# Sorting the rotated features of q and k into two chunks, and gathering the score operands in pieces

## The chip, the cores and the metric

The kernel runs on one core of a Trainium2 chip. The metric is the device time of one execution in microseconds (us). Three runs of the kernel before gave 603.58, 604.00 and 606.18 us, so its median is 604.0 us.

## The reference

It is a decoder trunk of two layers on one sequence of 256 tokens with 1024 features, all in float32. Only the first sub-layer, softmax attention with partial rotary, is touched. With 256 tokens there is one key block, so the block selection falls away and plain causal attention is left:

```python
xn = rmsnorm(h, attn_norm)                     # (1, 256, 1024)
q, k, v = split(xn @ w_qkv)                    # 16 heads of 64 features each
# partial rotary: only features 0..15 of a head's 64 are rotated
x1, x2, rest = x[..., :8], x[..., 8:16], x[..., 16:]
x = concat([x1 * cos - x2 * sin, x2 * cos + x1 * sin, rest])      # for q and for k
s = (q * 64**-0.5) @ k.T ; s = where(causal, s, -inf)
h = h + (softmax(s) @ v) @ w_o
```

A SwiGLU layer, an mLSTM mixer, another SwiGLU layer and a last norm follow. The order of the features within a head's q and k changes nothing in a score, as long as q and k have the same order.

## The kernel before

Float32 products are made of three matmuls on high and low parts: each weight tile `raw` (128x1024, 512 KB) is read by SP's queue, ScalarE casts its high part `wh`, VectorE subtracts the low part `wl`, and TensorE multiplies high by high, high by low and low by high (`mm3`). Four `raw` buffers and eight pairs `wh`, `wl` run ahead of TensorE; a load of `raw` waits until the `wl` of the tile four before it is made.

The attention has three stretches. First, `first_block` computes the first four 128-feature blocks of q and k ("chunks" 0 to 3, one PSUM bank each: k in one half, q in the other). Then the stream `main` runs: a list of generators gives TensorE one step at a time, and a queue of small jobs is kept by step number. A step is six matmuls of 256 columns or three of 512, whatever the generator. The generators stand in this order (`ORDER`): 16 steps of v for heads 0 to 7, 8 steps each of chunks 4, 5 and 6, `V1` steps of v for heads 8 to 15, 8 steps of chunk 7, the rest of v, then 28 steps of the output projection. After the stream one unit of 4 steps is left, so it is 96 steps in all.

Jobs are set by step numbers. Chunk c goes through `rotary`, then `stacks`; here a chunk holds two whole heads. `rotary` shuffles on VectorE, multiplies by the cosine table `Cr` on VectorE and by the sine table `Sr` on GpSimd, and adds on GpSimd. `stacks` copies the high part to a tile `u` on ScalarE, subtracts the low part on VectorE and gathers, with three DMAs for each head on SP's queue, a tile `stk` whose 128 rows hold high and low parts above each other (64 rows each, so a score needs two matmuls over 128 rows). Head h then has `scores` (S, four matmuls, at step 26 + 3h), `softmax`, `exps`, `recip`, `normalize` (VectorE and ScalarE in turn), `transposes` (T, three matmuls, 8 steps after the scores), `halves` and `lows_p`, and `values` (V, four matmuls, 14 steps after the scores).

VectorE, ScalarE and TensorE execute this stretch in the order in which the jobs were called; in the kernel before SP's order comes from a planner. Each engine works its list strictly in order: an instruction that waits holds everything behind it. The four PSUM banks of the tag `ps` are shared by the chunks' results, S, T and V; a chunk's bank is free once its `rotary` has read it, a head's S bank once `softmax` has.

Of the kernel before, what the change touches and what calls it, by code (L numbers as in the profile page):

```python
# [9 lines left out]
F32 = mybir.dt.float32  # L10
F32R = mybir.dt.float32r
# [5 lines left out]
P = 128  # L17
S = 256
# [4 lines left out]
LOOK = 4  # L23
A_LOOK = 4
ORDER = (0, 4, 5, 6, 1, 7, 1)
V1 = 4
WBUFS = 8
RAW = 4
LAG = 6
WARM = 16  # L30

A_D1, A_X, A_D2, A_N, A_D3, A_L, A_D4, A_O1, A_O2 = 0.5, 1, 3, 1, 1, 1.5, 0.5, 1, 1
A_O3, A_D5, A_D6, A_E, A_R, A_S, A_S2, A_W = 1, 2, 0, 1, 5, 6, 1.5, 1
A_START, A_STEP, A_T, A_V = 26, 3.0, 8, 14
M_START, M_STEP, M_A, M_B, M_C, M_G2, M_G3 = 32, 5, 1.5, 12, 22, 23, 28


C_COS, C_SIN, C_AMASK, C_ID = 0, 256, 512, 768
# [42 lines left out]
def trunk_kernel(ctx: ExitStack, tc: tile.TileContext, x, w, wg, fw, tab, out):  # L81
    nc = tc.nc
# [23 lines left out]
    vector_scalar = {mybir.EngineType.DVE, mybir.EngineType.Activation}  # L106
# [20 lines left out]
    tab_t = const.tile([P, C_END], F32, name="tab_t")  # L127
# [53 lines left out]
    tcos = tab_t[:, C_COS:C_COS + S]  # L181
# [252 lines left out]
    n = n0 = Norm(V_ATTN)  # L434
# [45 lines left out]
    with ExitStack() as actx:  # L480
        ap = actx.enter_context(tc.tile_pool(name="attn", bufs=3))
        ap1 = actx.enter_context(tc.tile_pool(name="attn1", bufs=1))

        Cr = ap1.tile([P, S], F32, name="Cr")
        Sr = ap1.tile([P, S], F32, name="Sr")
        nc.gpsimd.tensor_mul(Cr, tcos, n.R)
        nc.gpsimd.tensor_mul(Sr, tsin, n.R)
        pad(ap1, 16)
        VT = ap1.tile([P, 2, 16, P], F32R, name="VT")
        swap = [8 + i if i < 8 else i - 8 if i < 16 else i for i in range(32)]  # L490
        st = {}

        def rotary(hp, bank):
            b3 = bank.rearrange("p (g t) -> p g t", g=2)
            qk = ap.tile([P, 512], F32, name="qk", tag="qk", bufs=2)
            sh = ap.tile([P, 512], F32, name="sh", tag="sh", bufs=2)
            qk3, sh3 = (a.rearrange("p (g t) -> p g t", g=2) for a in (qk, sh))
            nc.vector.stream_shuffle(sh, bank, swap)
            nc.vector.tensor_mul(qk3, b3, Cr.unsqueeze(1).to_broadcast([P, 2, S]))  # L499
            nc.gpsimd.tensor_mul(sh3, sh3, Sr.unsqueeze(1).to_broadcast([P, 2, S]))  # L500
            nc.gpsimd.tensor_add(qk, qk, sh)

            def stack():
                st[hp] = stacks(ap, qk, 3, later=lambda f: main.later(A_S2, lambda: (f(), stacked.add(hp))))
            main.later(A_S, stack)

        evicted = set()
        stacked = set()
# [19 lines left out]
        pr = {}  # L528

        def scores(h):  # L530
            T = st[h // 2][:, h % 2]
            sc = ps_tile()
            dots(sc[:, 0:P], T, 0, P, 0, P)
            dots(sc[:, P:384], T, P, P, 0, S)
            main.later(A_D1, softmax, h, sc)
# [87 lines left out]
        def qk(hp):  # L623
            b = ps_tile()
            yield from pair_block("aqk", hp, n, b)
            main.later(A_D5, rotary, hp, b)

        acc = []
        blocks = [tok_block("av", 2 * i, n, v_evict, lambda *a: main.later(A_D6, *a)) for i in range(2)]
        parts = {0: [blocks[0]], 1: [islice(blocks[1], V1), blocks[1]]}  # L630
        main = Stream(*[(always, parts[i].pop(0) if i < 4 else qk(i)) for i in ORDER],
                      ((lambda: 0 in ot and 1 in ot), out_start(acc, "ao", ot)), *[((lambda hp=hp: hp in ot), out_steps(acc, "ao", hp, ot)) for hp in range(2, 7)])
        for hp in range(4):
            main.at(A_R * hp, rotary, hp, banks[hp])
# [294 lines left out]
def _tables():  # L929
    import numpy as np  # L930

    t = np.zeros((P, C_END), np.float32)
    pos = np.arange(S, dtype=np.float32)
    inv = np.float32(500000.0) ** (-np.arange(0, 16, 2, dtype=np.float32) / np.float32(16))
    ang = pos[:, None] * inv.astype(np.float32)[None, :]
    cos, sin = np.cos(ang).T, np.sin(ang).T
    t[:, C_COS:C_COS + S] = 1.0
    for h in (0, 64):
        t[h:h + 8, C_COS:C_COS + S] = cos
        t[h + 8:h + 16, C_COS:C_COS + S] = cos  # L940
        t[h:h + 8, C_SIN:C_SIN + S] = -sin
        t[h + 8:h + 16, C_SIN:C_SIN + S] = sin
    i, j = np.arange(P)[:, None], np.arange(P)[None, :]
    t[:, C_AMASK + P:C_AMASK + S] = np.where(j <= i, 0.0, -1e30)
    t[:, C_ID:C_ID + P] = np.eye(P)
    t[:, C_EMASK:C_EMASK + S] = np.tile(np.where(i <= j, 0.0, -30000.0), (1, 2))
    t[:, C_TRIU:C_TRIU + P] = i <= j
    t[:, C_TRIS:C_TRIS + P] = i > j
    for h in range(8):
        t[h, C_ID2 + h] = 1.0  # L950
        t[32 + h, C_ID2 + h] = 1.0
    return t


def _chunks(d):
    import numpy as np

    def cols(a, c0, c1):
        return a[:, c0:c1].reshape(8, P, c1 - c0).transpose(1, 0, 2)

    def pair(a, ca, cb, h):
        u = np.stack([cols(a, ca, ca + P), cols(a, cb, cb + P)], axis=2)
        return u[:, 4 * h:4 * h + 4].reshape(P, 1024)

    def wide(a, c0, i, h):
        k = (i % 2) * 4 + h * 2
        return cols(a, c0 + (i // 2) * 512, c0 + (i // 2) * 512 + 512)[:, k:k + 2].reshape(P, 1024)

    def rows(a, i, h):
        return a[(2 * i + h) * P:(2 * i + h + 1) * P]  # L970

    wq, wo = d["attn_w_qkv"][0], d["attn_w_o"][0]
    wi, wu = d["mlstm_w_in"][0], d["mlstm_w_out"][0]
    out = []
    pairs = {"aqk": (wq, 1024, 0), "mqk": (wi, 0, 512)}
    for l in range(2):
        pairs[f"gu{l}"] = (d["ffn_w_gate_up"][l], 0, 2816)
    for n, i, h in unit_names():
        if n.endswith("*"):
            a, ca, cb = pairs[n[:-1]]  # L980
            c = np.stack([a[i * P:(i + 1) * P, c0:c0 + 512].reshape(P, 4, P) for c0 in (ca, cb)], axis=2)
            c = c.reshape(P, 1024)
        elif n in pairs:
            a, ca, cb = pairs[n]
            c = pair(a, ca + i * P, cb + i * P, h)
# [12 lines left out]
        out.append(c)  # L998
    return np.stack(out)
# [32 lines left out]
```

## Time and profile before

| what | us |
|---|---|
| median of 3 runs | 604.0 |
| profiled execution | 604.25 |
| its span, first to last instruction | 602.5 |
| TensorE busy | 587.8 (98%) |
| VectorE busy | 415.6 (69%) |
| ScalarE busy | 340.3 (56%) |
| GpSimd busy | 71.0 (12%) |
| mean granted TensorE clock | 0.998 |

1.75 us of the profiled execution lie outside the span. Rows of a timeline give start, duration, engine, line, operation, output and inputs, the count of merged instructions, and in brackets how long the engine was idle before and what released it. The durations of pipelined matmuls overlap, so the time that one costs is read from the start of one row to the start of the next.

### The profile page before, as it was taken

How to read it: one execution, taken by the hardware profiler on the slowest of the kernel's cores; microseconds unless marked ns; L12 is line 12 of the kernel's file. 1: busy time of each engine (PE TensorE's matmuls, PEld its weight loads, DVE VectorE, ACT ScalarE, POOL GpSimd, SP SyncE). 2: the span in 40 equal slices, each digit the busy share in tenths (PEclk: the TensorE clock that was granted, in tenths of full speed). 3: DMA queues.
4: the chain of work that ended last, by engine and by line, in shares of the span. 5: the costliest groups of instructions: out<-in, count | busy, mean ns of one | idle time of the engine just before them, and what ended most of it. 6: DMA issues, size and time to landing. Idle time of an engine off the chain costs nothing.

```text
span 602.5 us, 11621 instructions
## 1 busy us (share of the span) xinstructions
PE 587.8 (98%) x4536; PEld 557.4 (93%) x4536; DVE 415.6 (69%) x674; ACT 340.3 (56%) x615; POOL 71.0 (12%) x77
## 2 busy tenths in 40 slices
PE   8997999999999999999999999999999999999995
PEld 7987888999999999999999878999999999999984
DVE  5999798796866666565487768868785656656522
ACT  7655899766644444445275467846664444444412
POOL 0464420041000000000032300113100000000000
PEclk9999999999999999999999999999999999999999
DMA  8869985458655556555428868332854555555401
GB/s 299 310 216 268 242 207 159 143 177 303 218 200 185 206 182 205 184 203 184 168 73 290 256 217 226 130 141 90 297 208 175 201 183 195 191 201 185 140 0 70
DMA packets 36630, 116.39 MB, mean 193 GB/s; under 512 B 4576, under 2 KB 7904, under 8 KB 36576
## 3 DMA queue, kind: packets, MB, share of 16 engines
q1 hardware_dynamic: 36144, 115.19, 58.3%
q8 instruction: 35, 0.57, 0.4%
q10 hardware_dynamic: 432, 0.47, 0.2%
q14 instruction: 19, 0.16, 0.1%
HBM read 105.15 MB, written 1.05 MB: 176 GB/s over the span
## 4 chain that ended last, share of the span: by engine, by line
PE 75%; DMA 8%; DVE 7%; ACT 5%; issue 3%; SPq 2%; POOLq 0%; POOL 0%; ACTq 0%; DVEq 0%
PE ps L191 43%; PE acc L191 31%; DMA raw<-w 4%; DMA stk<-u 3%; DVE wl L154 3%; ACT wh L164 1%; DVE u L462 1%; SPq L465 1%; SPq L466 1%; ACT xh L211 1%; ACT p L548 1%; DMA XV<-x 1%; PE ps L568 0%; ACT u L458 0%; DVE qk L499 0%
## 5 line engine op out<-in xcount | busy, mean ns | idle before, releaser
L154 DVE TENSOR_TENSOR wl<-raw,wh 128x1024 fp32r<-128x1024 f32 (+1 forms) x200 | 243.5, 1223 | 109.6 <-ACT wh L164 109.2
L164 ACT CAST wh<-raw 128x1024 fp32r<-128x1024 f32 (+1 forms) x200 | 205.6, 1034 | 178.0 <-PE ps L191 96.1
L191 PE MATMUL ps<-xh,wh 128*128 128x256 f32 x864 | 240.6, 278 | 0.0
L191 PE MATMUL ps<-xh,wl 128*128 128x256 f32 x864 | 239.5, 277 | 0.7 <-DVE wl L154 0.7
L191 PE MATMUL ps<-xl,wh 128*128 128x256 f32 x864 | 239.3, 277 | 0.0
L191 PEld LDWEIGHTS ps<-xh,wh 128*128 128x128 f32 x864 | 162.7, 188 | 1.4 <-ACT wh L164 0.4
L191 PEld LDWEIGHTS ps<-xh,wl 128*128 128x128 f32 x864 | 162.4, 188 | 1.2 <-DVE wl L154 1.1
L191 PEld LDWEIGHTS ps<-xl,wh 128*128 128x128 f32 x864 | 162.6, 188 | 0.7
L191 PE MATMUL acc<-hh,wh 128*128 128x256 f32 x176 | 48.6, 276 | 0.0
L191 PE MATMUL acc<-hl,wh 128*128 128x256 f32 x176 | 48.6, 276 | 0.0
L191 PE MATMUL acc<-hh,wl 128*128 128x256 f32 x176 | 48.6, 276 | 0.0
L657 DVE TENSOR_TENSOR tgu<-ps,R 128x512 f32<-128x512 f32 x42 | 28.6, 690 | 19.0 <-PE ps L191 19.0
L191 PE MATMUL acc<-wh,xh 128*128 128x512 f32 x96 | 39.0, 406 | 0.0
L225 POOL TENSOR_TENSOR ssum<-ssum,sq 128x512 f32<-128x512 f32 x9 | 16.2, 1806 | 186.9 <-issue 163.7
L191 PE MATMUL acc<-wh,xl 128*128 128x512 f32 x96 | 37.8, 393 | 0.0
L191 PE MATMUL acc<-wl,xh 128*128 128x512 f32 x96 | 37.7, 393 | 0.0
L191 PE MATMUL acc<-wh,hh 128*128 128x512 f32 (+1 forms) x92 | 35.5, 386 | 0.6 <-DVE yout L422 0.5
L191 PE MATMUL acc<-wh,hl 128*128 128x512 f32 (+1 forms) x92 | 35.4, 384 | 0.0
L191 PE MATMUL acc<-wl,hh 128*128 128x512 f32 (+1 forms) x92 | 35.3, 384 | 0.0
L191 PEld LDWEIGHTS acc<-hh,wh 128*128 128x128 f32 x176 | 33.0, 188 | 0.0
L191 PEld LDWEIGHTS acc<-hl,wh 128*128 128x128 f32 x176 | 33.0, 188 | 0.0
L191 PEld LDWEIGHTS acc<-hh,wl 128*128 128x128 f32 x176 | 33.0, 188 | 0.0
(182 smaller groups left out, 854.1 us busy)
## 6 DMA issues: line engine op xcount, KB each, us to landing
raw<-w SPq DMA_DIRECT2D x194, 512.0 KB, 4.2
stk<-u SPq DMA_DIRECT2D x24, 192.0 KB, 4.5
stk<-u SPq DMA_DIRECT2D x24, 128.0 KB, 4.3
stk<-u SPq DMA_DIRECT2D x24, 64.0 KB, 3.5
XV<-x SPq DMA_DIRECT2D x6, 128.0 KB, 5.8
tab_t<-tab SPq DMA_DIRECT2D x1, 708.0 KB, 7.3
raw<-w SPq DMA_DIRECT2D x4, 128.0 KB, 3.7
raw<-w SPq DMA_DIRECT2D x2, 256.0 KB, 4.6
```

The costliest lines, as they stand in the source:

```text
L154: nc.vector.tensor_sub(wl[:, sl], raws[c][:, sl], wh[:, sl].bitcast(F32))
L164: nc.scalar.copy(wh[:, sl], raws[c][:, sl])
L191: nc.tensor.matmul(o, lhsT=lhsT, rhs=rhs, start=start, stop=stop, skip_group_check=True)
L211: nc.scalar.activation(self.h[:, f], X[:, f], AF.Copy, scale=wc)
L225: eng.tensor_add(self.ssum, self.ssum, sq)
L462: nc.vector.tensor_sub(u[:, 512:1024], mv, u[:, 0:512].bitcast(F32))
L465: nc.sync.dma_start(out=st[0:64, hh].bitcast(F32), in_=u[r, 0:768].bitcast(F32))
L466: nc.sync.dma_start(out=st[64:128, hh, 0:512].bitcast(F32), in_=u[r, 512:1024].bitcast(F32))
L548: nc.scalar.activation(pt[:, sl], pt[:, sl], AF.Exp, bias=mx[:, t:t + 1], scale=-1.0, accum_out=ss[:, t:t + 1])
L657: nc.vector.tensor_mul(t.rearrange("p (g t) -> p g t", g=2), bank.rearrange("p (g t) -> p g t", g=2), n.R2())
```

## The change

The columns of the q and k weights are sorted on the host. Of each half of the heads (0 to 7, 8 to 15) the 16 rotated features of all eight heads come first and fill one chunk (chunks 0 and 4), and the 48 others of the eight heads fill three (1 to 3, 5 to 7). `rotary` needs the shuffle and four VectorE operations for chunks 0 and 4 alone; the other six chunks take one multiply. GpSimd has no part in it any more.

A head's rows now lie in two or three chunks, so its tile (`stz`, one of seven fixed tiles, in place of `stk`) is gathered in two or three pieces of 16, 32 or 48 rows with two DMAs each: 18 pieces for eight heads, 72 DMAs in place of 48. The last quarter of a tile's lower half is zero, which leaves out the product of the two low parts.

Scores stand at step 18 + 3.5h in place of 26 + 3h. The first part of v for heads 8 to 15 has 8 steps in place of 4 (`V1`), and chunk 7 comes 4 steps later. SP joins the engines that work in the order of the calls.

```diff
-A_O3, A_D5, A_D6, A_E, A_R, A_S, A_S2, A_W = 1, 2, 0, 1, 5, 6, 1.5, 1
-A_START, A_STEP, A_T, A_V = 26, 3.0, 8, 14
+A_O3, A_D5, A_D6, A_E, A_S, A_S2, A_S3, A_W = 1, 0.5, 0, 1, 1.5, 1.5, 2, 1
+A_R = (0, 2, 5, 8)
+A_START, A_STEP, A_T, A_V = 18, 3.5, 8, 14
+NT = 7
-        nc.gpsimd.tensor_mul(Cr, tcos, n.R)
-        nc.gpsimd.tensor_mul(Sr, tsin, n.R)
+        nc.vector.tensor_mul(CS, tab_t[:, C_COS:C_COS + 2 * S].rearrange("p (g t) -> p g t", g=2), n.R2())
+        stz = [ap1.tile([P, 768], F32R, name=f"stz{i}") for i in range(NT)]
+        for T in stz:
+            nc.gpsimd.memset(T[64:128, 512:768].bitcast(F32), 0.0)
+        def segments(h):
+            c, j = h // 8 * 4, h % 8
+            yield c, 16 * j, 16, 0
+            r, to = 48 * j, 16
+            while to < 64:
+                m = min(64 - to, P - r % P)
+                yield c + 1 + r // P, r % P, m, to
+                r, to = r + m, to + m
+            if c % 4:
+                nc.vector.tensor_mul(qk3, b3, n.R2())
+            else:
+                sh = ap.tile([P, 512], F32, name="sh", tag="qk", bufs=2)
+                nc.vector.stream_shuffle(sh, bank, swap)
+                nc.vector.tensor_mul(qk3, b3, Cr.unsqueeze(1).to_broadcast([P, 2, S]))
+                nc.vector.tensor_mul(sh3, sh3, Sr.unsqueeze(1).to_broadcast([P, 2, S]))
+                nc.vector.tensor_add(qk, qk, sh)
+            main.later(A_S, stack_high, c, qk)
+        def stack_high(c, qk):
+            u = ap.tile([P, 1024], F32R, name="u", tag="u", bufs=3)
+            nc.scalar.copy(u[:, 0:512], qk)
+            main.later(A_S2, stack_low, c, qk, u)
+        def stack_low(c, qk, u):
+            nc.vector.tensor_sub(u[:, 512:1024], qk, u[:, 0:512].bitcast(F32))
+            parts[c] = u
+            ...
+                    main.when(main.pos + d, lambda h=h: h < NT or h - NT in scored, stack, h)
+        def stack(h):
+            T = stz[h % NT]
+            for c, r, m, to in segments(h):
+                v = parts[c][r:r + m].bitcast(F32)
+                nc.sync.dma_start(out=T[to:to + m].bitcast(F32), in_=v[:, 0:768])
+                nc.sync.dma_start(out=T[64 + to:64 + to + m, 0:512].bitcast(F32).rearrange("p (b c) -> p b c", c=S),
+                                  in_=v.rearrange("p (b c) -> p b c", c=S)[:, 0::3])
-        with tc.manual_schedule(engines=vector_scalar):
+        with tc.manual_schedule(engines=vector_scalar | {mybir.EngineType.SP}):
```

SP's list early in the stream. Before, a weight load stands after each chunk's six DMAs of `stk`; the last row is the load of the stream's eleventh weight tile:

```order
L145 DMA raw_562<-w 128x1024
L467 DMA stk_558<-u_556 64x256 x2
L465 DMA stk_558<-u_556 64x768
L466 DMA stk_558<-u_556 64x512
L465 DMA stk_558<-u_556 64x768
L466 DMA stk_558<-u_556 64x512
L145 DMA raw_597<-w 128x1024
```

In the change, the last piece DMAs of the first seven heads (`stz_478` is head 6's tile, `stz_472` that of heads 0, 7 and 14), the load of the same eleventh weight tile, and what follows:

```order
L543 DMA stz_478<-u 16x768
L544 DMA stz_478<-u 16x2x256
L543 DMA stz_478<-u 48x768
L544 DMA stz_478<-u 48x2x256
L147 DMA raw<-w 128x1024
L543 DMA stz_472<-u 16x768
L544 DMA stz_472<-u 16x2x256
L543 DMA stz_472<-u 48x768
L544 DMA stz_472<-u 48x2x256
L147 DMA raw<-w 128x1024 x5
```

From head 0's first piece to the eleventh tile's load there are 32 piece DMAs and two other weight loads; before, 12 DMAs of `stk` and one load stand there.

ScalarE's list from the first copy to `u` on, before (`exps` are the L548 rows):

```order
L458 CAST u<-qk 128x512 [waits Pool_49]
L164 CAST wh<-raw 128x1024 [waits DMAHW4_49,Activation_49]
L458 CAST u<-qk 128x512 [waits Pool_49]
L164 CAST wh<-raw 128x1024 [waits DMAHW5_49,PE_49,Activation_49]
L458 CAST u<-qk 128x512 [waits DMAHW3_49,DMAHW2_49,DMAHW4_49,DMAHW1_49,DMAHW7_49,DMAHW0_49,Pool_49]
L164 CAST wh<-raw 128x1024 [waits DMAHW6_49,PE_49]
L517 ACTIVATE VT<-acc,r 128x4x2x64 [waits PE_49] x2
L164 CAST wh<-raw 128x1024 [waits DMAHW5_49]
L458 CAST u<-qk 128x512 [waits DMAHW3_49,DMAHW2_49,DMAHW6_49,DMAHW1_49,DMAHW7_49,DMAHW0_49,Pool_49]
L164 CAST wh<-raw 128x1024 [waits DMAHW4_49]
L548 ACTIVATE p,ss<-p,mx 128x256 [waits DVE_49]
```

And in the change (`exps` are the L591 rows):

```order
L527 CAST u<-qk 128x512 [waits DVE_49]
L166 CAST wh<-raw 128x1024 [waits DMAHW4_49,Activation_49]
L527 CAST u<-qk 128x512 [waits DMAHW2_49,DMAHW1_49,DMAHW5_49,DMAHW0_49,DMAHW6_49,DVE_49,Activation_49]
L166 CAST wh<-raw 128x1024 [waits PE_49] x2
L559 ACTIVATE VT<-acc,r 128x4x2x64 [waits PE_49,Pool_49]
L559 ACTIVATE VT<-acc,r 128x4x2x64 [waits PE_49]
L591 ACTIVATE p,ss<-p,mx 128x256 [waits DVE_49]
L591 ACTIVATE p,ss<-p,mx 128x128 [waits DVE_49]
L166 CAST wh<-raw 128x1024 [waits DMAHW1_49]
L591 ACTIVATE p,ss<-p,mx 128x256 [waits DVE_49]
L591 ACTIVATE p,ss<-p,mx 128x128 [waits DVE_49]
```

The copies to `u` of chunks 2 and 3 are the first and third of these rows. There are three `u` tiles. In both kernels the copy of a fourth chunk waits for DMAs that read an earlier one (DMAHW names the semaphore of a DMA); in the change all four copies stand ahead of the `VT` copies and of the first `exps`, and the fourth waits for the pieces of heads 0, 1 and 2 that come out of chunk 1.

## Rows read from the trace of the kernel before

**Rows 1.** The page's first part: busy us, share of the span and instructions.

```profile
PE 587.8 (98%) x4536; PEld 557.4 (93%) x4536; DVE 415.6 (69%) x674; ACT 340.3 (56%) x615; POOL 71.0 (12%) x77
```

**Rows 2.** Windows: stretch, length, busy us of each engine, clock, DMA share, GB/s.

```profile
45.00:60.00 15.00, 11.28 (x94) 10.65 (x93) 14.65 (x32) 8.57 (x18) 6.05 (x5) 1.00 0.91 270
```

**Rows 3.** Timeline of TensorE: the stream's first matmul and three that waited.

```profile
29.45 0.39 PE L191 MATMUL acc<-wh,xh 128*128 128x512 f32 x1
...
53.94 0.69 PE L191 MATMUL ps<-stk 128*128 128x128 f32 x4 [1.42 <-issue]
...
58.40 0.84 PE L568 MATMUL ps<-tab_t,p 128*128 128x128 f32 x3 [2.24 <-ACT p L558]
...
69.41 0.83 PE L568 MATMUL ps<-tab_t,p 128*128 128x128 f32 x3 [0.98 <-DVE qk L499]
```

**Rows 4.** Chain of waits, late attention: start us, us, what.

```profile
101.60 0.41 PE ps L191 x4
...
102.01 0.35 PE ps L568 x3
...
103.06 0.46 PE ps L191 x4
...
116.27 7.55 PE acc L191 x66
```

**Rows 5.** Timeline of VectorE, 27 to 54 us.

```profile
27.62 0.76 DVE L498 STREAM_SHUFFLE sh<-ps 128x512 f32<-128x512 f32 x1
...
36.20 2.32 DVE L154 TENSOR_TENSOR wl<-raw,wh 128x1024 fp32r<-128x1024 f32 x1
...
48.11 1.65 DVE L520 SCALAR_TENSOR_TENSOR VT<-acc,r,VT 128x256 fp32r<-128x256 f32 x4
...
49.68 1.21 DVE L154 TENSOR_TENSOR wl<-raw,wh 128x1024 fp32r<-128x1024 f32 x1
...
53.18 0.66 DVE L499 TENSOR_TENSOR qk<-ps,Cr 128x512 f32<-128x512 f32 x1
...
53.77 0.40 DVE L542 CUSTOM_DVE_ANT_0 p<-ps,tab_t 128x256 f32<-128x256 f32 x1
```

**Rows 6.** Timeline of ScalarE, 44 to 58 us.

```profile
44.31 1.26 ACT L517 ACTIVATE VT<-acc,r 128x512 fp32r<-128x512 f32 x2
...
48.61 0.62 ACT L458 CAST u<-qk 128x512 fp32r<-128x512 f32 x1 [2.09 <-DMA stk<-u]
...
54.22 0.51 ACT L548 ACTIVATE p<-p,mx 128x256 f32<-128x256 f32 x1 [3.76 <-DVE mx L542]
...
55.60 1.05 ACT L164 CAST wh<-raw 128x1024 fp32r<-128x1024 f32 x1 [0.40 <-DMA raw<-w]
...
57.95 0.80 ACT L558 ACTIVATE p<-p,ss 128x128 f32<-128x128 f32 x2
```

**Rows 7.** Timeline of GpSimd.

```profile
35.81 1.62 POOL L501 TENSOR_TENSOR qk<-qk,sh 128x512 f32<-128x512 f32 x1
```

**Rows 8.** Timeline of SP's queue: an issue is its row's duration.

```profile
3.79 0.33 SPq L143 DMA_DIRECT2D XV<-x  x1
...
50.81 0.59 SPq L466 DMA_DIRECT2D stk<-u  x1
...
51.45 0.60 SPq L467 DMA_DIRECT2D stk<-u  x1
...
335.44 1.18 SPq L466 DMA_DIRECT2D stk<-u  x1
```

**Rows 9.** DMA issues, 30 to 60 us: count, KB each, median us to landing.

```profile
raw<-w SPq DMA_DIRECT2D x8, 512.0 KB, 4.1
```

**Rows 10.** The tile stk, 34 to 56 us: its DMAs.

```profile
DMA to landing us min/median/max: 2.4/3.0/3.8
```

**Rows 11.** Timeline of TensorE at the start.

```profile
1.12 3.59 PE L118 MATMUL acc<-warm 128*128 128x256 bf16 x16 [1.12 <-POOL warm L115]
...
6.20 0.28 PE L191 MATMUL ps<-xh,wh 128*128 128x256 f32 x1
```

More of the change, by code (lines that the diff above doesn't have):

```diff
@@ L25 @@
 ORDER = (0, 4, 5, 6, 1, 7, 1)
-V1 = 4
+V1 = 8
 WBUFS = 8
@@ L482, in trunk_kernel @@
         ap1 = actx.enter_context(tc.tile_pool(name="attn1", bufs=1))
-        Cr = ap1.tile([P, S], F32, name="Cr")
-        Sr = ap1.tile([P, S], F32, name="Sr")
-        nc.gpsimd.tensor_mul(Cr, tcos, n.R)
-        nc.gpsimd.tensor_mul(Sr, tsin, n.R)
+        CS = ap1.tile([P, 2, S], F32, name="CS")
+        nc.vector.tensor_mul(CS, tab_t[:, C_COS:C_COS + 2 * S].rearrange("p (g t) -> p g t", g=2), n.R2())
+        Cr, Sr = CS[:, 0], CS[:, 1]
         pad(ap1, 16)
         VT = ap1.tile([P, 2, 16, P], F32R, name="VT")
-        swap = [8 + i if i < 8 else i - 8 if i < 16 else i for i in range(32)]
+        stz = [ap1.tile([P, 768], F32R, name=f"stz{i}") for i in range(NT)]
@@ L491, in trunk_kernel @@
+        for T in stz:
+            nc.gpsimd.memset(T[64:128, 512:768].bitcast(F32), 0.0)
+        swap = [i ^ 8 for i in range(32)]
         st = {}
-        def rotary(hp, bank):
+        parts = {}
+        scored, valued = set(), set()
+        def segments(h):
[6 more added lines that the diff above has]
+                r, to = r + m, to + m
@@ L494, in rotary @@
+        def rotary(c, bank):
             b3 = bank.rearrange("p (g t) -> p g t", g=2)
             qk = ap.tile([P, 512], F32, name="qk", tag="qk", bufs=2)
[L496 to L505, printed above, removed]
+            qk3 = qk.rearrange("p (g t) -> p g t", g=2)
+            if c % 4:
+                nc.vector.tensor_mul(qk3, b3, n.R2())
+            else:
+                sh = ap.tile([P, 512], F32, name="sh", tag="qk", bufs=2)
+                sh3 = sh.rearrange("p (g t) -> p g t", g=2)
+                nc.vector.stream_shuffle(sh, bank, swap)
+                nc.vector.tensor_mul(qk3, b3, Cr.unsqueeze(1).to_broadcast([P, 2, S]))
+                nc.vector.tensor_mul(sh3, sh3, Sr.unsqueeze(1).to_broadcast([P, 2, S]))
+                nc.vector.tensor_add(qk, qk, sh)
@@ new lines, in rotary @@
+            main.later(A_S, stack_high, c, qk)
[6 more added lines that the diff above has]
+            parts[c] = u
+            d = A_S3
+            for h in range(c // 4 * 8, c // 4 * 8 + 8):
+                if max(g[0] for g in segments(h)) == c:
+                    main.when(main.pos + d, lambda h=h: h < NT or h - NT in scored, stack, h)
+                    d += 1
@@ L507, in trunk_kernel @@
+        def stack(h):
[5 more added lines that the diff above has]
+                                  in_=v.rearrange("p (b c) -> p b c", c=S)[:, 0::3])
+            st[h] = T
+            stacked.add(h)
         evicted = set()
@@ L530, in scores @@
         def scores(h):
-            T = st[h // 2][:, h % 2]
+            T = st.pop(h)
+            scored.add(h)
             sc = ps_tile()
@@ L586, in values @@
             hp, hh = h // 2, h % 2
+            valued.add(h)
             if hh == 0:
@@ L629, in trunk_kernel @@
         blocks = [tok_block("av", 2 * i, n, v_evict, lambda *a: main.later(A_D6, *a)) for i in range(2)]
-        parts = {0: [blocks[0]], 1: [islice(blocks[1], V1), blocks[1]]}
-        main = Stream(*[(always, parts[i].pop(0) if i < 4 else qk(i)) for i in ORDER],
+        order = {0: [blocks[0]], 1: [islice(blocks[1], V1), blocks[1]]}
+        main = Stream(*[(always, order[i].pop(0) if i < 4 else qk(i)) for i in ORDER],
                       ((lambda: 0 in ot and 1 in ot), out_start(acc, "ao", ot)), *[((lambda hp=hp: hp in ot), out_steps(acc, "ao", hp, ot)) for hp in range(2, 7)])
         for hp in range(4):
-            main.at(A_R * hp, rotary, hp, banks[hp])
+            main.at(A_R[hp], rotary, hp, banks[hp])
         for h in range(16):
             s0 = A_START + A_STEP * h
-            main.when(s0, lambda h=h: h // 2 in stacked, scores, h)
-            main.when(s0 + A_T, lambda h=h: h in pr, transposes, h)
-            main.when(s0 + A_V, lambda h=h: h in pT and h // 8 in evicted, values, h)
-        with tc.manual_schedule(engines=vector_scalar):
+            main.when(s0, lambda h=h: h in stacked and len(scored) == h, scores, h)
+            main.when(s0 + A_T, lambda h=h: h in pr and h - len(valued) < 3, transposes, h)
+            main.when(s0 + A_V, lambda h=h: h in pT and h // 8 in evicted and (h % 2 == 0 or h // 2 in pair), values, h)
+        with tc.manual_schedule(engines=vector_scalar | {mybir.EngineType.SP}):
             wlag[0], look[0] = A_W, A_LOOK
@@ L936, in _tables @@
     cos, sin = np.cos(ang).T, np.sin(ang).T
-    t[:, C_COS:C_COS + S] = 1.0
-    for h in (0, 64):
+    for h in range(0, P, 16):
         t[h:h + 8, C_COS:C_COS + S] = cos
@@ L970, in rows @@
         return a[(2 * i + h) * P:(2 * i + h + 1) * P]
+    f = np.arange(1024).reshape(2, 8, 64)
+    f = np.concatenate([f[:, :, :16].reshape(2, P), f[:, :, 16:].reshape(2, 3 * P)], axis=1).reshape(-1)
     wq, wo = d["attn_w_qkv"][0], d["attn_w_o"][0]
+    wq = wq[:, np.concatenate([f, 1024 + f, np.arange(2048, 3072)])]
     wi, wu = d["mlstm_w_in"][0], d["mlstm_w_out"][0]
```

## The prediction

> **What bounds the kernel now.** I read the busy times, then TensorE's timeline in the attention, then what the other engines did ahead of each wait. TensorE is busy for 98% of the span [rows 1], so only its waits can be won. Inside the attention stream it stood still 1.42, 2.24 and 0.98 us at three places [rows 3]. To know how much can be won in all, I set the stream's length against its work. Eleven steps cost 7.55 us, 0.69 each; a head's scores cost 0.46, its transposes 0.35, its values 0.41 [rows 4]. So 96 steps and 16 heads are 66.2 + 19.5 = 85.7 us. The stream began at 29.45 [rows 3] and its last matmul run began at 116.27 and took 7.55 [rows 4], so it took 94.4: 8.7 us are waits and slow restarts. No change that leaves TensorE's work alone can gain more here than that, and this one leaves it alone.
>
> What made the waits is one thing. From 45 to 60 us VectorE was busy 14.65 of 15 us [rows 2]. The score of head 2 started at 53.94, right as the multiply of chunk 4 ended (53.18 + 0.66) [rows 3, 5]: it waited for that chunk's PSUM bank. Head 0's `softmax` came at 53.77 [rows 5], ScalarE had waited 3.76 us for it [rows 6], and head 0's transposes stood 2.24 us for `normalize` (57.95 + 0.80) [rows 3, 6]. VectorE was late because a low part took 2.32 us beside GpSimd's add and 1.21 without [rows 5, 7].
>
> **The change part by part.** *VectorE and GpSimd.* GpSimd's two operations of each chunk go, and the time VectorE lost beside them (2.32 - 1.21 = 1.1 us in such a low part) goes too. Chunks 0 and 4 get a multiply and an add more, the table one multiply, the six others lose the shuffle. All are 128x512 operations that start 0.59 us apart (53.18 to 53.77) [rows 5]; 5 more and 6 fewer come to nothing. The zero fills stand at the head of GpSimd's list, where it idles. VectorE is then no longer the late engine. I find two things that are later instead.
>
> *First, the fourth copy to `u`.* On ScalarE it stands ahead of two casts, both `VT` copies and head 0's `exps`, and it waits until the pieces of heads 0 to 2 taken out of chunk 1 have landed. When is that? VectorE starts the shuffle at 27.62 [rows 5]. Then come 0.6 for it, 0.6 table, 1.2 low part, 1.8 for the rest of chunk 0, 0.6 for chunk 1, 0.25 until chunk 0's copy is made, 0.7 for its low part, 1.2, 0.6, and 0.7 for chunk 1's low part: 35.9. Then SP can issue head 0's third DMA; its first two went out before. The last of those chunk-1 pieces is ten issues later. DMAs of `stk` follow each other by 0.64 us (50.81 to 51.45) [rows 8], whatever their size in this trace. No row has a piece of 16 rows or a pattern like `16x2x256`. From below, the shortest issue is 0.33 [rows 8], 0.38 with the same gap; from above, the longest of a `stk` DMA is 1.18 [rows 8]. I take 0.64, the same kind of transfer, SBUF to SBUF. So 42.4, and 3.0 to land [rows 10]: 45.4. ScalarE then needs 0.6 (copy), 2.0 (two casts) and 1.2 (`VT`) [rows 6]; VectorE, whose fourth low part waits behind the same copy, makes the `VT` low parts by 50.4 and `softmax` of head 0 by 51.0 (1.65 and 0.6) [rows 5]; then `exps` 0.95, the cast of the next weight 0.95, `exps` of head 1 0.95, `normalize` 0.75 give 54.6 to 55.2; I take 55. TensorE wants head 0's transposes earlier. Scores of head 0 at step 18: 29.45 + 18 x 0.69 = 41.9; head 1 four steps on, 45.1; head 2 three steps on, 47.6; transposes one step on: 48.8. **Wait: 6.2 us**, most of it already in head 2's score, which finds chunk 4, chunk 5 and the scores of heads 0 and 1 in the four banks until that `softmax`. Such a wait of a copy to `u` for DMAs is in the trace, 2.09 us long [rows 6]; there two `exps` did not stand behind it.
>
> *Second, the eleventh weight tile.* Its load stands behind 32 pieces and two loads; from head 0's third DMA that is 32 issues, 35.9 + 20.5 = 56.4, and 4.1 to land [rows 9]: 60.5. ScalarE's cast of it stands ahead of `exps` of head 2 and `normalize` of head 1. Cast 1.0, copy of chunk 4 0.55, `exps` 0.95, copy of the transposes 0.35, `normalize` 0.75: 64.1. TensorE wants head 1's transposes at 55.0 + 0.35 + 3 steps + 0.46 + 1 step = 58.6. **Wait: 5.5 us.** The tile itself is not late for its own matmuls (step 40).
>
> *The rest.* After that SP is free to run ahead, five loads follow at once, and ScalarE's list for a head (cast, two `exps`, two `normalize`, copies; some 3.5 us) fits in the 3.5 steps and 1.22 us that TensorE needs for one (3.6). Heads 13 to 15 now need chunk 7, which ends eight steps before head 13's score, and the chain multiply, copy, low part, two issues, landing is some 9 us against 5.5 of steps and 2 of other heads: 1 us, by the lag. The second `VT` block and two late `normalize` come to some 2 us, as the small waits do before. I take 3 us, bounds 1 and 6.
>
> *Sum.* 6.2 + 5.5 + 3 = 14.7 us of waits, 8.7 before: +6.0. The profiled execution took 604.25 us, 0.25 over the median of 604.0, so 610.25 against it and **610 us** against the median. Everything behind the attention is the same list of instructions; its first loads are issued as before.
>
> The Trainium skill, "DMA: Bandwidth & Descriptors", section "Rules for kernel authors", says that many small transfers should be coalesced, since under 64 KB one pays mostly overhead. By that rule the new pieces of 32 and 48 KB cost what larger ones do, and the sum stands as it is. The page gives no time for an issue; the flat 0.64 us of the trace agrees with it down to 64 KB and shows nothing below.
>
> **The rivals.** *Faster: pieces issue cheaply.* A quarter of the rows might be issued in less time. At 0.38 us a piece the fourth copy goes at 42.7 and head 0's transposes at 52.3; the eleventh tile lands at 52.2, and head 1 waits for nothing. Waits: 3.5 + 0 + 1 to 3, so 4.2 to 2.2 less than before: 600 to 602. It decides at some 0.45 us, where 9 us of waits are left; at 0.5 it is 605. For it: loads from HBM issue in 0.33. Against: sizes from 64 to 192 KB made no difference.
>
> *All waits go.* If the copies to `u` do not wait as I read it, the eight steps of earlier start hide every chain and only the last 3 us stay: 604 - 5.7 = 598. Against it stands the list itself.
>
> *TensorE's clock falls in the gaps.* It granted 1.00 (2.4 GHz) over 45 to 60 us with a gap of 2.24 [rows 2, 3]. A gap of 5.5 us is nowhere in the trace. At the start, after standing idle, 16 matmuls of 256 columns took 3.59 us, 0.22 each, and full pace (0.11) came at 6.20 [rows 11]. The same again after one or both gaps costs half of 5.1 us each: 612.5 to 615. The Trainium skill, "TensorE: Matmul & The Clock Gate", Part 1, says that an idle array falls back to 1.2 GHz; by that rule this is what would happen, and the trace neither shows nor excludes it.
>
> *Pieces issue slowly.* If every second piece (the `16x2x256` kind) takes 1.18, the eleventh tile is 9 us later: some 619.
>
> **How the numbers follow.** The forecast (606 to 613) 0.48; cheap pieces (600 to 605.5) 0.26; all waits gone 0.08; a fallen clock (613 to 616) 0.13; slow pieces 0.05. A difference under 0.5%, 3 us, can't be told from none. Faster, under 601: 0.08 and nearly half of the cheap pieces, 0.20. Within 3 us: the rest of them and a tenth of the forecast, 0.20. Slower: 0.60. The range leaves out all waits gone and the slowest pieces: 600.5 to 616, since cases of both signs hold much of the chance.
>
> **What would show it.** Right: ScalarE idle from some 37 us to 45 us ahead of a copy to `u`, released by a DMA of `stz`; head 0's transposes at 54 to 56 us; a cast idle until a load issued at 56 us lands; head 1's transposes near 64; piece DMAs 0.6 us apart. GpSimd idle through the attention and low parts of 1.2 us throughout. Wrong: a first transpose before 52 us, pieces under 0.45 us apart, or a stream that ends before 124 us.

## The result and the profile after

The changed kernel takes 612.35 us, the median of 4 runs (612.13 to 613.71); the kernel before took 604.88 us beside it (4 runs, 603.58 to 606.18). The medians are 7.5 us apart. The ratio on record, which isn't the quotient of these two medians, is 1.0145, with a 95% interval of 1.0121 to 1.0169: slower, by some 8 us. The forecast was 610, in a range of 600.5 to 616. The profiled execution took 612.19 us with a span of 610.4, against 604.25 for the one before.

The first part of the page of the changed kernel, answering to [rows 1]: busy time, share of the span, instructions.

```profile
PE 591.1 (97%) x4536; PEld 560.5 (92%) x4536; DVE 408.5 (67%) x667; ACT 340.2 (56%) x615; POOL 45.6 (7%) x66
```

TensorE has a lower share than before, though it has the same 4536 matmuls. So the place to look is its timeline in the attention stream, answering to [rows 3]. L611 is a head's transposes.

```profile
50.12 0.72 PE L193 MATMUL ps<-stz 128*128 128x128 f32 x4 [2.49 <-DVE mx L585]
53.05 1.09 PE L611 MATMUL ps<-tab_t,p 128*128 128x128 f32 x3 [1.50 <-ACT p L601]
64.37 1.09 PE L611 MATMUL ps<-tab_t,p 128*128 128x128 f32 x3 [6.03 <-ACT p L601]
```

The bracket is how long TensorE stood, and for what: 2.49 us ahead of head 2's scores, 1.50 ahead of head 0's transposes, 6.03 ahead of head 1's. The last matmul run of the stream, in the chain of waits, starts 8.5 us later than the 116.27 of [rows 4]:

```profile
124.77 7.55 PE acc L193 x66
```

The stream begins at 29.23 and ends at 124.77 + 7.55 = 132.32. That is 103.1 us against 94.4 before, for the same 85.7 us of work: 17.4 us beyond that work where there were 8.7. The whole loss lies here; the span grew by 7.9.

What came late is on ScalarE's timeline, answering to [rows 6].

```profile
44.33 0.62 ACT L527 CAST u<-qk 128x512 fp32r<-128x512 f32 x1 [7.82 <-DMA stz<-u]
...
50.78 1.03 ACT L166 CAST wh<-raw 128x1024 fp32r<-128x1024 f32 x1
...
61.20 1.04 ACT L166 CAST wh<-raw 128x1024 fp32r<-128x1024 f32 x1 [7.81 <-DMA raw<-w]
...
63.92 0.80 ACT L601 ACTIVATE p<-p,ss 128x128 f32<-128x128 f32 x2
```

ScalarE stands twice for nearly 8 us: ahead of the fourth copy to `u` (released by a piece's DMA), and ahead of the cast of the eleventh weight tile (released by that tile's load). Head 1's `normalize` stands behind that cast in order, so its transposes wait for a weight tile that they have no use for.

Why the load is late is on SP's queue, answering to [rows 8]: L543 and L544 are the two DMAs of a piece, L147 a weight tile's load, and the duration is the issue.

```profile
45.28 0.59 SPq L543 DMA_DIRECT2D stz<-u  x1
45.91 0.64 SPq L544 DMA_DIRECT2D stz<-u  x1
46.59 0.59 SPq L147 DMA_DIRECT2D raw<-w  x1
...
55.70 1.53 SPq L544 DMA_DIRECT2D stz<-u  x1
57.73 0.33 SPq L147 DMA_DIRECT2D raw<-w  x1
```

The row at 46.59 is the tenth tile's load, that at 57.73 the eleventh's. SP issues from 36 to 56 us without a break, one DMA in 0.6 to 0.7 us. 14 piece DMAs lie between the two loads.

The last thing is TensorE's clock. The windows of the changed kernel give length, TensorE's busy time (matmuls), granted clock, share and rate of the DMA engines:

```profile
64.00:66.00 2.00, 1.63 (x7) 0.50 0.95 379
66.00:68.00 2.00, 2.00 (x11) 0.50 0.92 371
68.00:70.00 2.00, 2.00 (x13) 0.56 0.72 242
70.00:72.00 2.00, 1.94 (x18) 1.00 0.27 84
```

After the 6.03 us of idleness the granted clock is 0.50, the lower of the two levels (1.2 GHz). It comes back by 70 us. Little more than half as many matmuls fit in the time.

VectorE was relieved as the change says. Groups by line and shape, 30 to 126 us: the low parts of the weights take 1218 ns in the mean (before: 1405 over 30 to 118 us), those of `u` 686 (before: 1048).

```profile
L156 DVE TENSOR_TENSOR wl<-raw,wh 128x1024 fp32r<-128x1024 f32 x21 | 25.5, 1218 | 7.2 <-ACT wh L166 7.1
...
L531 DVE TENSOR_TENSOR u<-qk,u 128x512 fp32r<-128x512 f32 x8 | 5.5, 686 | 7.0 <-ACT u L527 7.0
```

### The profile page after: what moved, and what is told of

The parts are those of the page before. It is cut to its first block, busy times and chain, and to the rows that moved or that the text cites. A ratio compares the mean times of both kernels' runs of the same rounds, so it can differ in the third digit from the quotient of the medians.

```text
span 610.4 us, 11611 instructions
## 1 busy us (share of the span) xinstructions
PE 591.1 (97%) x4536; PEld 560.5 (92%) x4536; DVE 408.5 (67%) x667; ACT 340.2 (56%) x615; POOL 45.6 (7%) x66
## 4 chain that ended last, share of the span: by engine, by line
PE 86%; SPq 4%; ACT 3%; DMA 3%; DVE 2%; issue 2%; POOLq 0%; POOL 0%; DVEq 0%; ACTq 0%
PE ps L193 49%; PE acc L193 35%; SPq L544 2%; SPq L543 2%; DMA raw<-w 1%; PE ps L611 1%; ACT p L591 1%; DMA stk<-u 1%; ACT wh L166 1%; DMA XV<-x 1%; DVE wl L156 0%; DMA stz<-u 0%; ACT p L601 0%; PE acc L727 0%; ACT ph L617 0%
## 5 line engine op out<-in xcount | busy, mean ns | idle before, releaser
L156 DVE TENSOR_TENSOR wl<-raw,wh 128x1024 fp32r<-128x1024 f32 (+1 forms) x200 | 239.1, 1202 | 113.5 <-ACT wh L166 113.1
```

What stands on the lines that cost most here:

```text
L156: nc.vector.tensor_sub(wl[:, sl], raws[c][:, sl], wh[:, sl].bitcast(F32))
```

## The experiments

Three theories. A: SP's issue rate. Pieces at 0.64 us each hold back the tenth and eleventh weight loads, and ScalarE works in order. B: the copy of chunk 3 to `u` waiting for one of three buffers is a cost of its own, added to the first (so the prediction's sum had it). C: the clock that falls after the gaps costs what the sum left out.

One table first, so that each run can be read against the others. "Head 0" and "head 1" are the starts of their transposes, counted from the first matmul of the stream; "behind" is from head 1's transposes to the stream's end. All come from TensorE's timeline and the chain of waits of one profile each. A profile is of one run, and that run can lie off the median of its kernel: by 1.9 us below in e7, by 1.3 below in e2 and e4, by 1.1 and 1.2 above in e8 and e10. The ratio is to the kernel before, timed beside it.

| kernel | head 0 | head 1 | behind | stream | median us | ratio, 95% interval |
|---|---|---|---|---|---|---|
| before | 28.95 | 32.20 | 62.2 | 94.4 | 603.7 to 604.9 | 1 |
| changed | 23.8 | 35.1 | 67.95 | 103.1 | 612.35 | 1.0145, 1.0121 to 1.0169 |
| e1, four buffers of u | 23.7 | 34.7 | 67.8 | 102.5 | 612.83 | 1.0148, 1.0117 to 1.0180 |
| e2, half the piece DMAs | 21.6 | 26.5 | 65.8 | 92.3 | 604.40 | 1.0017, 0.9992 to 1.0041 |
| e3, TensorE kept at work | 24.1 | 35.1 | 66.3 | 101.5 | 610.49 | 1.0116, 1.0078 to 1.0154 |
| e4, chunk 3's step later | 25.3 | 32.3 | 65.75 | 98.0 | 609.09 | 1.0078, 1.0047 to 1.0110 |
| e5, e1 + pieces just in time | 19.7 | 24.5 | 69.0 | 93.5 | 603.23 | 0.9992, 0.9972 to 1.0011 |
| e6, e1 + half from GpSimd | 22.85 | 28.05 | 65.8 | 93.8 | 604.43 | 1.0019, 0.9998 to 1.0040 |
| e7, e5 and e6 | 20.35 | 24.0 | 65.4 | 89.4 | 600.64 | 0.9957, 0.9936 to 0.9977 |
| e8, heads from step 26 | 38.4 | 42.9 | 59.6 | 102.5 | 611.47 | 1.0135, 1.0105 to 1.0165 |
| e9, half from GpSimd | 25.5 | 30.9 | 65.5 | 96.4 | 605.66 | 1.0030, 1.0015 to 1.0046 |
| e10, e7 from step 16 | 21.45 | 25.8 | 72.4 | 98.2 | 608.28 | 1.0071, 1.0052 to 1.0091 |

**e1: a fourth buffer for u.** The space comes from `CS` made in place in the table, one `o` and one `p` buffer less.

```diff
-            u = ap.tile([P, 1024], F32R, name="u", tag="u", bufs=3)
+            u = ap.tile([P, 1024], F32R, name="u", tag="u", bufs=4)
```

> A fourth buffer for u, so that the copy of chunk 3 to u waits for no piece; every engine's list stays as it is. Theory A (the issue rate of SP holds back the tenth and the eleventh weight tile, and ScalarE stands in order behind their casts): the copy goes at 37 to 38 us instead of 44.33, but the tenth tile's load is still issued near 46.6 and cast near 50.7, so head 0's transposes stay at 52.5 to 53.5 us; the eleventh's load stays near 57.7 and head 1's transposes near 64.4. Time 612.3, within 1.5. Theory B (the prediction's: the copy's wait is a cost of its own that adds to the other): head 0's transposes at 49 to 50, the stream 4 us shorter, 607 to 609.

ScalarE's timeline, and TensorE's at the two transposes:

```profile
37.55 0.61 ACT L527 CAST u<-qk 128x512 fp32r<-128x512 f32 x1
...
51.80 1.04 ACT L166 CAST wh<-raw 128x1024 fp32r<-128x1024 f32 x1 [4.84 <-DMA raw<-w]
...
61.86 1.04 ACT L166 CAST wh<-raw 128x1024 fp32r<-128x1024 f32 x1 [7.44 <-DMA raw<-w]
```
```profile
54.08 1.09 PE L611 MATMUL ps<-tab_t,p 128*128 128x128 f32 x3 [4.15 <-ACT p L601]
65.03 1.09 PE L611 MATMUL ps<-tab_t,p 128*128 128x128 f32 x3 [4.86 <-ACT p L601]
```

The copy now waits for nothing, and the time doesn't move. ScalarE gives the 7 us back ahead of later casts, 3.15 us at the ninth tile's and 4.84 at the tenth's: that tile's load is issued at 47.76, and its cast can go only at 51.8. This stream began 1.1 us later for reasons ahead of it; counted from its start, head 0's transposes come 23.7 us in, as in the changed kernel. B falls as an addition. The wait of 7.82 us in the changed kernel's profile was real and cost nothing by itself, since a second one ran beside it and ended at the same time. (e1 also has one `o` and one `p` buffer less, so what shows nothing is the whole edit.)

**e2: half the piece DMAs.**

```diff
-            nc.gpsimd.memset(T[64:128, 512:768].bitcast(F32), 0.0)
+            nc.gpsimd.memset(T[64:128].bitcast(F32), 0.0)
...
                 nc.sync.dma_start(out=T[to:to + m].bitcast(F32), in_=v[:, 0:768])
-                nc.sync.dma_start(out=T[64 + to:64 + to + m, 0:512]...
```

> Leaves out the DMA of each piece's lower half (one of the three products of the scores is zero): 36 piece DMAs instead of 72, lists otherwise the same. Theory A (0.64 us an issue): the tenth tile's load goes near 41, the eleventh's near 47 us, the fourth copy near 39.5; head 0's transposes at 48 to 50, head 1's not later than 59, no low clock; stream 10 to 12 us shorter: 600 to 602.5. Rival (the waits come from landing times and from ScalarE's own list, not from the number of issues): over 608.

In the changed kernel 256 of the 768 columns of a tile's lower half are zero, a third of it; here all are.

SP's loads of the tenth and the eleventh tile, ScalarE's fourth copy and its cast of the tenth tile, and TensorE (the transposes are on L609 in this kernel):

```profile
41.41 0.59 SPq L147 DMA_DIRECT2D raw<-w  x1
46.45 0.53 SPq L147 DMA_DIRECT2D raw<-w  x1
```
```profile
42.47 0.62 ACT L527 CAST u<-qk 128x512 fp32r<-128x512 f32 x1 [5.64 <-DMA stz<-u]
...
48.92 1.03 ACT L166 CAST wh<-raw 128x1024 fp32r<-128x1024 f32 x1
```
```profile
51.18 0.84 PE L609 MATMUL ps<-tab_t,p 128*128 128x128 f32 x3 [1.50 <-ACT p L599]
56.03 0.84 PE L609 MATMUL ps<-tab_t,p 128*128 128x128 f32 x3 [0.79 <-ACT p L599]
```

Both loads go when A said (41 and 47), the clock stays at 1.00, and the stream is 10.8 us shorter. Head 0 is 1.2 us later than the 50 at most that I gave, and the time is 1.9 us above the 602.5: the fourth copy went at 42.47 and not near 39.5, held by a piece's DMA, and the cast of the tenth tile behind it waited for nothing. With the loads early, the copy sets head 0. The loss against the kernel before is gone with half of the issues.

**e3: TensorE kept at work in the gaps.**

```diff
+            if h == 2:
+                keep(20)
...
+            if h < 2:
+                keep((12, 52)[h])
```

`keep(k)` is k matmuls of the warm-up tile into a free PSUM bank.

> 84 dummy matmuls of 256 columns (20 ahead of head 2's scores, 12 and 52 ahead of the transposes of heads 0 and 1) keep TensorE at work where it stands idle. Theory C (the clock that falls after the gaps costs 3.8 us): granted clock 1.00 from 52 to 72 us, head 1's transposes still near 64.4 but the matmuls behind them 0.115 us apart: 608 to 609.5. Rival (the slow stretch only takes the place of waits that come anyway, or the clock falls for another reason): the clock stays below 0.8 or the time within 1 us of 612.3.

The windows after head 1's transposes:

```profile
64.00:66.00 2.00, 1.69 (x13) 1.00 0.93 346
66.00:68.00 2.00, 2.00 (x19) 1.00 1.02 381
```

The clock stays up, and 19 matmuls run in 2 us where 11 did. But the stream wins only 1.6 us, and the interval of the time overlaps that of the changed kernel: half of what I expected. The table says why. In the changed kernel the clock also fell between heads 0 and 1 (0.67 over 52 to 54 us, 0.50 over 54 to 56), and there it cost nothing: with full clock head 1's transposes still come 35.1 us in, since the load sets them. Only the slow stretch behind head 1 costs. C is right in kind and half in size, as far as one profile shows; the times alone don't part e3 from the changed kernel.

**e4: chunk 3's step later.** The copy of chunk 3 moves from 1.5 to 13 steps behind its `rotary` (step 8), so by 11.5 steps and not by the seven that the expectation counts.

```diff
-            main.later(A_S, stack_high, c, qk)
+            main.later(13 if c == 3 else A_S, stack_high, c, qk)
```

> The step that copies chunk 3 to u and issues the pieces of heads 5 and 6 is put seven steps later: the copy stands behind head 0's exps, and the eleventh and twelfth weight tiles' loads ahead of these ten pieces. Theory A: the tenth tile still gates normalize of head 0 (transposes at 52.5 to 53.5), the eleventh's load goes near 52 and lands near 56, head 1's transposes at 59 to 60.5 instead of 64.37: 605 to 608. Theory B (the copy's wait for its buffer was what made head 0 late): head 0's transposes at 49 to 50, and head 1's follow with them.

ScalarE (`exps` of head 1, the copy of chunk 4), then TensorE:

```profile
53.48 0.51 ACT L591 ACTIVATE p<-p,mx 128x256 f32<-128x256 f32 x1 [1.10 <-DVE mx L585]
...
59.53 0.62 ACT L527 CAST u<-qk 128x512 fp32r<-128x512 f32 x1 [3.43 <-DMA stz<-u]
```
```profile
54.82 1.09 PE L611 MATMUL ps<-tab_t,p 128*128 128x128 f32 x3 [5.77 <-ACT p L601]
61.76 0.84 PE L611 MATMUL ps<-tab_t,p 128*128 128x128 f32 x3 [1.61 <-ACT p L601]
```

The eleventh load goes at 50.24 and head 1 comes 2.9 us earlier; behind it the clock is at full and 2.2 us more are won. Head 0 is not earlier (B), it is 1.5 us later, which A hadn't foreseen either. The moved low part stands ahead of head 1's `softmax` on VectorE, and head 1's `exps`, which ScalarE has ahead of head 0's `normalize`, wait 1.10 us for it. Head 1 came at 61.8 and not at 59 to 60.5 for another reason: the eleventh tile was in time, but ScalarE has the copy of chunk 4 ahead of head 1's `normalize`, and that copy waited 3.43 us for a piece's DMA. With the load early, a wait of the fourth copy's kind is what holds head 1. The time missed the 608 by a microsecond.

**e5: pieces at most eight steps ahead of their head**, with the four buffers of e1. With three buffers this order isn't possible, since the fourth copy would wait for pieces that wait for it.

```diff
-                    main.when(main.pos + d, lambda h=h: ...
+                    main.when(max(main.pos + d, A_START + A_STEP * h - 8), lambda h=h: ...
```

> The kernel with four buffers for u, and the pieces of a head issued eight steps ahead of its scores at the earliest, not as soon as its chunks are there. No DMA less, but SP's queue has the tenth weight tile's load behind 8 pieces (18 before) and the eleventh's behind 14 (32 before). Theory A (what costs is which load stands behind how many pieces at 0.64 us each): tenth load near 40, eleventh near 45 us; head 0's transposes at 49 to 50.5, head 1's at 54 to 56, granted clock 1.00, 85.7 us of work plus 3 to 6 of waits: 598 to 602. Rival (SP's total work or ScalarE's list binds as before): head 1's transposes after 60, over 607.

```profile
49.15 0.49 PE L611 MATMUL ps<-tab_t,p 128*128 128x128 f32 x3
...
53.90 0.49 PE L611 MATMUL ps<-tab_t,p 128*128 128x128 f32 x3
...
93.42 0.70 PE L193 MATMUL ps<-stz 128*128 128x128 f32 x4 [2.81 <-DMA stz<-u]
```

Not one DMA less, and neither transpose waits: which load stands behind how many pieces is what counts. Both transposes come where A had them, within 0.1 us. The time is that of before, though, 1.2 us over my 602: a new wait of 2.81 us comes at 93 us. Head 13 waits there for its last piece, which SP issues at 88.7, after 1.5 us of waiting for chunk 7's low part. It lands 4.4 us later, and the six piece DMAs issued from 84 to 89 us take 7.0 us to land in the median: three weight loads had been issued just ahead of them, at 82.42.

**e6 and e7: the second DMA of each piece from GpSimd's queue**, in the order of e1, and in that of e5.

```diff
-                nc.sync.dma_start(out=T[64 + to:64 + to + m, 0:512]...
+                nc.gpsimd.dma_start(out=T[64 + to:64 + to + m, 0:512]...
```

> Four buffers for u, and the second DMA of each piece issued from GpSimd's queue instead of SP's; order otherwise as in the changed kernel. Theory A (SP's issue rate): tenth load near 41, eleventh near 46 us as with half the pieces, head 0's transposes at 48.5 to 50, head 1's before 57: 599 to 603. Rival (GpSimd issues more slowly than one in 1.3 us, or its DMAs disturb VectorE): scores wait for DMAs of stz, low parts over 1.5 us, over 606.

> Both together: four buffers, pieces at most eight steps ahead, second DMAs from GpSimd. Theory A: little more than either alone, since the waits on loads are gone with one of them: 598 to 602, waits at transposes under 2 us in all. Rival: the issue rate still costs something in the one with SP alone, then 2 us or more under it.

In e6 SP's tenth load, ScalarE's cast of that tile and TensorE, then TensorE in e7 with the last run of its stream:

```profile
42.41 0.33 SPq L147 DMA_DIRECT2D raw<-w  x1
```
```profile
49.77 1.05 ACT L166 CAST wh<-raw 128x1024 fp32r<-128x1024 f32 x1 [2.58 <-DMA raw<-w]
```
```profile
43.51 0.70 PE L193 MATMUL ps<-stz 128*128 128x128 f32 x4 [1.79 <-DMA stz<-u]
...
52.04 0.84 PE L611 MATMUL ps<-tab_t,p 128*128 128x128 f32 x3 [1.35 <-ACT p L601]
57.24 0.84 PE L611 MATMUL ps<-tab_t,p 128*128 128x128 f32 x3 [1.14 <-ACT p L601]
```
```profile
49.14 0.49 PE L611 MATMUL ps<-tab_t,p 128*128 128x128 f32 x3
52.76 0.49 PE L611 MATMUL ps<-tab_t,p 128*128 128x128 f32 x3
...
110.64 7.55 PE acc L193 x66
```

e6 wins back the loss, as e2 did, but its loads go at 42.4 and 49.4, later than the 41 and 46 that I gave, and head 0's scores wait 1.79 us for pieces: 1.4 us over my 603. The tenth tile is cast 7.4 us after its load's issue, 4.2 in the changed kernel (46.59 to 50.78), so most of what the earlier issue won for head 0 is lost in landing. e7 has no wait at any transpose and 0.7 us for pieces in all. Its stream is 89.4 us, 5 less than before, and it beats both kernels: 600.64 us, 0.4% under the kernel before (interval 0.2% to 0.6%) and 1.9% under the changed one. It is 2.6 us under e5 in the median, the number of the rival named for e7 (2 us or more). That the issuing on SP alone costs this in e5 isn't shown: e5's longest wait is for a piece that landed late behind weight loads.

**e8: heads from step 26 again.**

```diff
-A_START, A_STEP, A_T, A_V = 18, 3.5, 8, 14
+A_START, A_STEP, A_T, A_V = 26, 3.0, 8, 14
```

> The changed kernel with the heads from step 26 in steps of 3, as before the change. Theory A: the pieces keep their place in SP's queue, the eleventh load is still issued near 57 and lands near 61; its cast now stands ahead of head 0's exps, so head 0's transposes come near 64 instead of a wanted 55, and head 1 waits for nothing: 608 to 611. Rival (the early heads make the waits; eight steps more cover every chain): 603 to 605, head 0's transposes before 57.

ScalarE, then TensorE:

```profile
62.42 1.04 ACT L166 CAST wh<-raw 128x1024 fp32r<-128x1024 f32 x1 [10.16 <-DMA raw<-w]
```
```profile
67.04 1.09 PE L611 MATMUL ps<-tab_t,p 128*128 128x128 f32 x3 [7.36 <-ACT p L601]
```

The rival that the early heads make the waits falls: with eight steps more, the eleventh load is issued at 58.7 (57.73 in the changed kernel) and head 0 waits for it in place of head 1. It comes at 67 and not 64: after the cast, ScalarE still had the copy of chunk 4, the `exps` of two heads and a cast ahead of head 0's `normalize`. The time is 0.5 us over my range.

**e9: GpSimd's queue with three buffers of u.**

> The second DMA of each piece from GpSimd's queue as in e6, but with the three buffers of u as changed. Theory A (SP's issue rate alone; the copy's wait costs nothing of its own while the tenth load comes as late): the fourth copy near 42.5, head 0's transposes at 50 to 52, head 1's at 56 to 58, as with half the pieces: within 2 us of e6. Theory B (the wait for the fourth buffer costs once SP is quick): head 0's transposes 3 us or more behind e6's 52.0 and the time over 607.

```profile
46.25 0.62 ACT L527 CAST u<-qk 128x512 fp32r<-128x512 f32 x1 [9.47 <-DMA stz<-u]
```
```profile
54.97 1.09 PE L611 MATMUL ps<-tab_t,p 128*128 128x128 f32 x3 [1.50 <-ACT p L601]
```

The time is within 2 us of e6, as A said. But the copy goes at 46 and not 42.5, head 0 comes at 55 and not at 50 to 52, head 1 at 60.4 and not at 56 to 58. Counted from the stream's start head 0 is 2.6 us later than in e6. That is under the 3 us of B, and the time is under B's 607, so neither line fits as a whole. With the loads early, the third buffer does cost at head 0, as in e2. How much of it is the buffer alone isn't shown, since the piece that the copy waits for also lands later with two queues (see the last section). The two waits run side by side, and the later one counts. In the changed kernel they ended together.

**e10: e7 with the heads from step 16.**

> e7 (four buffers, pieces at most eight steps ahead, second DMAs from GpSimd) with the heads from step 16 instead of 18. Theory A: e7's stream of 89.4 us holds 3.7 us of waits, none at a transpose, so an earlier start can win 1 us at most and may bring a wait for stz at head 0 (two steps, 1.4 us): 599 to 602, no different from e7. Rival: the last heads' chain still sets the end, and two steps less give 1 to 2 us: 598 to 599.5.

TensorE's timeline, and its windows in the columns used above:

```profile
41.76 0.70 PE L193 MATMUL ps<-stz 128*128 128x128 f32 x4 [1.71 <-DMA stz<-u]
...
93.57 0.69 PE L193 MATMUL ps<-stz 128*128 128x128 f32 x4 [1.87 <-DMA stz<-u]
...
96.43 1.19 PE L193 MATMUL ps<-stz 128*128 128x128 f32 x4 [1.21 <-DMA stz<-u]
```
```profile
44.00:48.00 4.00, 4.00 (x25) 0.66 1.06 286
...
92.00:96.00 4.00, 1.66 (x10) 0.82 0.89 242
96.00:100.00 4.00, 3.57 (x17) 0.50 0.76 209
```

A clear miss of both lines, 6 us over the wider one. Two steps less leave the pieces short three times (head 0 and two heads near 95 us, 4.8 us in all), and after the first of them, and again near 95 us, the clock falls. The stream is 8.8 us longer than e7's.

**What stays open.** e5 has every DMA of the changed kernel in another order and takes the time of the kernel before, so the order of SP's list, at 0.6 us an issue, made the loss. Its fourth buffer, without which that order isn't possible, gave nothing alone (e1). The change also took that order away from the planner; the new pieces in the planner's order were not run.

## Why the prediction was right, and where its terms were off

**What bounds it.** Right. All that was lost is in TensorE's waits and slow matmuls inside the stream: +8.7 us there, +7.9 in the span.

**VectorE at nothing.** Right: weights' low parts take 1.2 us throughout, GpSimd is idle from 30 to 118 us, and VectorE ends one long wait of TensorE, the 2.49 us ahead of head 2's scores, where its fourth low part had itself stood 6.96 us for the fourth copy. That its relief is worth something once nothing else is late is consistent with e7, but e7 also has the early heads; the two were not parted.

**The fourth copy, 6.2 us.** The mark was right and its cause only half. The copy came at 44.33 (forecast 45.4), released by a piece. Head 0's transposes came at 53.05 (55), so 4.5 us late against the wanted 48.8 (19.35 after the stream's start) and not 6.2. The step that failed is "the cast of the next weight 0.95" in the chain behind the copy: I gave that cast a duration and no load. Its load, the tenth tile's, stands behind 18 pieces: issued at 46.59, it lands at some 50.4, and the cast starts at 50.78. It holds head 0 just as long (e1). Taking one wait away shows nothing there (e1: same time); with the loads early, the copy's wait sets head 0 (e2; 2.6 us in e9 against e6).

**The eleventh weight tile, 5.5 us.** Right by every step: issue at 57.73 (forecast 56.4; one issue took 1.53 us), cast at 61.20 (60.5), transposes at 64.37 (64.1). Since head 0 was earlier than forecast and this load pins head 1, head 1 came 7.7 us behind its work and not 5.5 (TensorE stood 6.03 of them), and the sum up to there hardly moved: 12.2 us of waits to head 1's transposes (35.1 less the 22.95 us that the same work takes by the forecast), 11.7 forecast. e2, e4, e5 and e6, which each bring this load forward by another way, all bring head 1 forward.

**The rest, 3 us.** The size came, its causes didn't, and a term is missing beside it. Behind head 1 the forecast's work is 85.7 - 22.95 = 62.75 us. e2, e4 and e6 need 65.75 to 65.8 there at full clock: 3.0 more. The forecast meant waits: 1 us at heads 13 to 15, 2 at the second `VT` block and late `normalize`. But behind head 1's transposes the timelines of these runs have only 0.3 to 0.5 us of idle time in brackets, and the changed kernel one row:

```profile
102.66 0.70 PE L193 MATMUL ps<-stz 128*128 128x128 f32 x4 [0.49 <-DVE pl L622]
```

The other 2.5 us stand in no bracket: either the work is dearer than the prices taken from [rows 4], or gaps too short for a bracket add up; which of the two isn't shown. The kernel before has such time too, 8.7 us in the forecast's sum with some 5.4 in brackets. The waits that the forecast named didn't come, and that its 3 us fit all the same is luck.

The changed kernel needs 67.95 behind head 1. The other 2.2 us are the clock, which I had at nothing in the sum and as a rival at 2.55 a gap, 612.5 to 615. e3 gave 1.6 of them back. So the clock fell at both gaps, and the rival's price came for one of the two: 14.7 forecast + 0.5 up to head 1 + 2.2 of clock = 17.4 measured. The Trainium skill, "TensorE: Matmul & The Clock Gate", Part 1, says that an idle array goes back to 1.2 GHz; the 0.50 after 6.03 us agrees. Between heads 0 and 1 the slow stretch was free, since the eleventh load set head 1 anyway (e3), and that halved the price here.

**The sum.** 610 against 612.35, and in part by luck. The sum had the first wait 1.7 us too large and the second 2.2 too small, and it left the clock's 2.2 out. The rival of one gap with a fallen clock (612.5) is nearer to the measured time than the forecast.

**Cheap pieces.** Fell: 0.55 to 0.64 us an issue (median of the first DMA 0.580, of the second 0.636) for 32 to 144 KB, no cheaper for a quarter of the rows. **Slow pieces** fell too: of the second DMAs one took 1.53 us and one 1.22, the others 0.63 to 0.68. **All waits gone** fell with the first two brackets of the timeline.

## What to carry to other kernels

Count the issues of a queue, not its bytes: 32 small DMAs at 0.64 us put 20 us between a weight load and its turn, and an engine that works in order then passes that wait to work that has no use for the tile. When two waits end at about the same time, mending one shows nothing (e1); look for what stands next in the list before giving a wait a price. Issuing pieces no earlier than needed and sharing the issuing between two queues beat the kernel before together (e7); each alone only made good the loss.

## What the runs showed of the hardware that was not expected

A second queue takes issue time off SP, at a price in landing. Issues from GpSimd took 0.51 us (median of 36 in e7). But in 30 to 64 us the pieces landed after a median of 2.6 us in the changed kernel, 3.3 in e5 (one queue, other order), and 5.1 to 6.1 in e6, e7 and e9 (two queues). The Trainium skill, "DMA: Bandwidth & Descriptors", section "Rules for kernel authors", says that spreading DMAs over several engines' queues saves issue time alone, since all run on the same DMA engines. The runs agree: the issue time was saved (e6), and nothing was won in landing, where SP's own pieces, too, took a median of 6.2 us in e6. What part of the longer landing is GpSimd's kind of DMA and what part is more traffic at a time stays open.

The length of a gap doesn't tell by itself whether the clock falls. It stayed at 1.00 after 2.24 us in the kernel before [rows 2, 3] and 1.79 in e6, and fell after 1.71 in e10 (0.66 over 44 to 48 us).
